# Spreading 1/rms over the partitions: transposes placed by TensorE's order in the heads and between the layers of an encoder

## The chip, the cores and the metric

The kernel runs on one NeuronCore of a Trainium2 chip. The metric is device time in microseconds for one execution, lower is better. A core has TensorE (PE: matrix products and transposes into the accumulation memory, PSUM), VectorE (DVE), ScalarE (ACT) and GpSimd (POOL) for work on rows of data, and SyncE (SP), whose queue issues nearly all DMAs here. Each engine works through its own queue in a fixed order; the engines wait for each other by semaphores.

## The reference

One encoder layer over two independent inputs of 512 tokens by 1024 channels, all in float32:

```python
x = x + 0.5 * swiglu(rms_norm(x, ffn1_norm), ffn1_w_gate, ffn1_w_up, ffn1_w_down)
h = rms_norm(x, mix_norm)
proj = h @ w_in                       # queries, keys, values, memory q k v, gates
att = gqa_block_attention(aq, ak, av)
mem = mlstm_bidirectional(mq, mk, mv, gate_pre, mlstm_gate_bias, o_pre, mlstm_head_norm)
merged = jax.nn.sigmoid(g_att) * (att @ w_up_att) + jax.nn.sigmoid(g_mlstm) * (mem @ w_up_mlstm)
x = x + merged @ w_out
x = x + 0.5 * swiglu(rms_norm(x, ffn2_norm), ffn2_w_gate, ffn2_w_up, ffn2_w_down)
return rms_norm(x, final_norm)

def rms_norm(x, g):
    y = x * lax.rsqrt(jnp.mean(x * x, axis=-1, keepdims=True) + EPS)
    return y * g
```

The mLSTM memory (4 heads of width 128, both directions) also ends in such a normalisation, per token and head: `h * rsqrt(mean(h * h) + EPS)`, times the head's gain and output gate.

## The kernel before

Data lies transposed: channels on the 128 partitions, 512 tokens along a row, so that a matrix of 1024 channels is eight tiles of 128 x 512. Both inputs ("streams" 0 and 1) are worked on together: the large products of the two feed-forward blocks and of the joint part of the input projection use seven products of half size for eight (B11, B21, T1 to T4, B22 in the code). Every float32 product is three matmuls over a high and a low part of each operand; a tile is split by a ScalarE copy (high) and a VectorE subtraction (low).

*The normalisation.* The mean of squares is over channels, that is over partitions. ScalarE squares a tile, and GpSimd or VectorE adds the eight squares into `acc`. `col_sums` (L174 to L181) turns `acc` by four TensorE transposes (L177) into a PSUM bank, so that each token has a partition, and VectorE reduces along the row (L179). `rstd_cols` adds the epsilon and takes the power -0.5, two small GpSimd steps (L165, L167). The result has one value per token, on the token's partition; to scale tiles with tokens along the row it must be spread over all partitions. `bcast_psum` (L183 to L188) does that by four more transposes (L187) of the column, broadcast to 128 x 128. `bcast_cols` copies the bank to a tile called R (L193). The banks come from a pool of two (`PT`, named pst in the profile), used in turn by all the transposes and by some products.

*The order.* The code is traced by Python in one sequence; a scheduler then gives each engine its queue, once and for all, before the kernel runs. It goes by the order of tracing as priority and by its own estimate of when each instruction's inputs are ready. `shifted(n)` sets the priority of what is traced inside it back by n (or forward, if n is negative). On the chip the queue's order does not change: TensorE stands still at an instruction whose inputs are not there, whatever waits behind it.

*Where the spreading stands.* There are fourteen. Two belong to the start of the first feed-forward block and are not touched. The others:

- R0 and R1, between the first block and the mixing part. R0 (stream 0) is made in `done1`, which the down projection `ffn_down` calls as each of its output tiles is complete (T4 gives the last tile of stream 0, then follow T1 and B22 with those of stream 1). It scales the eight tiles of stream 0 for `kv_proj` (L717). R1 is made after `k_rope` and used by `next_x1`, eight tiles along the attention loop.
- Eight memory heads, four of each stream. `mem_head` computes a head's scores (L1186, three matmuls for each of four blocks), weighs them with exponentials (ScalarE L1200, VectorE L1202), and at its end divides (L1214, L1215, L1217). `mem_out` transposes the weights (L1231), multiplies with the values (L1239), and at its end squares the result, makes the column sums, the spreading and the scaling of `og` (L1249) and splits it into `mem`. `steps` runs the two generators in turns, `mem_out` of one head against `mem_head` of the next, and calls `between` after each turn.
- R2 of both streams, between the mixing part and the second feed-forward block.

*Filler work.* Independent products are kept in units: a load (DMA, split of the weights) and a computation, run by `go` with one or two loads ahead. `first` holds the 14 units of the joint projection (24 matmuls each; two are given before `k_rope`, four among the four `q_rope` calls, the rest by `fill` in the attention loop). In the heads, `between` takes units from `queue`: the last joint product, eight merges of attention (24 matmuls), eight merges of memory (12) and eight output units (24) of stream 0. `pace` sets 7 units over the first 24 turns and 16 over the next 24.

## Time and profile before

| | |
|---|---|
| median of 3 runs | 2077.77 us (2076.35 to 2079.03) |
| the profiled execution | 2078.2 us, its span 2076.4 us |
| instructions | 27167, of them 9320 matmuls and transposes |
| DMA | 438.60 MB, 211 GB/s on average |
| granted TensorE clock, mean | 0.994 of full speed |

The span is the time from the first to the last instruction of one execution; what lies around it is the launch. In the lines of the profile PE is TensorE's matmuls and transposes, PEld its weight loads; a group is named by its line, engine and operation, and by what it writes and reads (`pst<-ident,rs` is a transpose of a tile of `rstd_cols` into a bank of `PT`). In brackets stands the idle time of the engine just before and what ended it. Where a helper is called from many places, all its calls have one line.

### The profile page before, as it was taken

Reading aid. Unit: us, or ns where it says so; the run is one execution under the profiler, and the core shown is the slowest. Engines: PE = TensorE matmul, PEld = TensorE weight load, DVE = VectorE, ACT = ScalarE, POOL = GpSimd, SP = SyncE. Lnnn points to the kernel's source line nnn. Section 1 sums busy time; section 2 is a strip of 40 time slices with the busy share of each in tenths; the row PEclk is TensorE's granted clock in tenths of the full one; section 3 lists DMA queues with packets and bytes.
Section 4 is the critical chain, followed back from the end, with each engine's and each line's share of the span. In section 5 each row is a group of like instructions: output and inputs, shape, how many; then the busy total and the mean of one; then the engine's idle time right before and its main releaser. Section 6 shows DMA issues by size and latency. Waiting matters only on the chain.

```text
span 2076.4 us, 27167 instructions
## 1 busy us (share of the span) xinstructions
PE 2036.5 (98%) x9320; PEld 1664.9 (80%) x9320; DVE 1652.3 (80%) x2802; ACT 954.3 (46%) x1763; POOL 135.4 (7%) x147
## 2 busy tenths in 40 slices
PE   8999999999999999999999998999999999999998
PEld 6888888888888777778887776878888888888887
DVE  6888888786798598669988688675888888786796
ACT  6544444442224565535555666444544444442222
POOL 1000000001002210010100110111000000000010
PEclk9999999999999999999999999999999999999999
DMA  8656555599765656664445775587656555598753
GB/s 281 198 176 198 193 172 183 189 338 365 273 214 208 204 159 206 219 205 143 139 140 165 259 229 159 170 255 218 212 175 197 193 172 183 190 347 343 274 188 117
DMA packets 332347, 438.60 MB, mean 211 GB/s; under 512 B 21072, under 2 KB 196192, under 8 KB 330416
## 3 DMA queue, kind: packets, MB, share of 16 engines
q1 hardware_dynamic: 331616, 435.60, 63.4%
q0 software_dynamic: 592, 1.27, 0.3%
q8 instruction: 73, 1.20, 0.2%
q14 instruction: 66, 0.54, 0.1%
HBM read 285.63 MB, written 151.16 MB: 210 GB/s over the span
## 4 chain that ended last, share of the span: by engine, by line
PE 86%; DVE 6%; DMA 4%; ACT 2%; issue 1%; POOL 1%; SPq 0%; DVEq 0%; POOLq 0%; ACTq 0%
PE mm L309 20%; PE pss L309 17%; PE pst L309 11%; PE mm L565 8%; PE mm L733 5%; PE pst L565 4%; PE pss L565 4%; PE mm L717 3%; PE pso L565 3%; PE pso L1059 1%; PE pst L1051 1%; PE pss L1032 1%; PE pss L717 1%; PE pst L733 1%; PE pss L1186 1%
## 5 line engine op out<-in xcount | busy, mean ns | idle before, releaser
L309 PE MATMUL mm<-xc,w 128*128 128x512 f32 x2064 | 514.2, 393 | 3.7 <-ACT w L267 2.1
L309 PEld LDWEIGHTS mm<-xc,w 128*128 128x128 f32 x2064 | 386.1, 188 | 84.6 <-ACT w L267 2.9
L309 PE MATMUL pss<-xc,w 128*128 128x512 f32 x1056 | 256.3, 391 | 0.3 <-DVE t L340 0.3
L309 PE MATMUL pst<-xc,w 128*128 128x512 f32 x1056 | 253.8, 389 | 0.0
L309 PEld LDWEIGHTS pss<-xc,w 128*128 128x128 f32 x1056 | 196.9, 188 | 47.5 <-DVE t L340 6.9
L309 PEld LDWEIGHTS pst<-xc,w 128*128 128x128 f32 x1056 | 198.2, 188 | 41.5 <-ACT t L344 0.4
L267 ACT ACTIVATE w<-t 128x512 fp32r<-128x512 f32 x232 | 141.5, 628 | 182.5 <-issue 55.2
L268 DVE TENSOR_TENSOR w<-t,w 128x512 fp32r<-128x512 f32 x232 | 157.2, 692 | 58.1 <-ACT w L267 55.7
L565 PE MATMUL mm<-rt,w 128*128 128x512 f32 (+1 forms) x819 | 189.2, 385 | 0.0
L565 PEld LDWEIGHTS mm<-rt,w 128*128 128x128 f32 x819 | 151.5, 188 | 29.7
L309 PE MATMUL pss<-xc,f 128*128 128x512 f32 x528 | 126.8, 389 | 0.0
L309 PEld LDWEIGHTS pss<-xc,f 128*128 128x128 f32 x528 | 99.1, 188 | 20.6
L634 ACT ACTIVATE w<-wr 128x512 fp32r<-128x512 f32 x72 | 45.1, 632 | 138.5 <-PE pso L565 70.9
L634 ACT ACTIVATE w<-t 128x512 fp32r<-128x512 f32 x82 | 51.6, 632 | 114.3 <-PE pst L565 69.0
L268 DVE TENSOR_TENSOR w<-wr,w 128x1024 fp32r<-128x1024 f32 x58 | 71.6, 1235 | 32.0 <-ACT w L267 31.9
L565 PE MATMUL pss<-rt,w 128*128 128x512 f32 x396 | 93.7, 389 | 0.0
L565 PE MATMUL pst<-rt,w 128*128 128x512 f32 x396 | 93.7, 389 | 0.0
L717 PE MATMUL mm<-w,xc 128*128 128x512 f32 (+1 forms) x432 | 91.2, 358 | 2.2 <-DVE xs L583 1.4
L565 PEld LDWEIGHTS pss<-rt,w 128*128 128x128 f32 x396 | 74.3, 188 | 15.4
L565 PEld LDWEIGHTS pst<-rt,w 128*128 128x128 f32 x396 | 74.3, 188 | 15.4
L267 ACT ACTIVATE w<-wr 128x1024 fp32r<-128x1024 f32 x58 | 61.4, 1058 | 50.2 <-PE pst L309 21.6
L717 PEld LDWEIGHTS mm<-w,xc 128*128 128x128 f32 x432 | 71.9, 188 | 14.1 <-DVE xs L583 1.6
(344 smaller groups left out, 3519.9 us busy)
## 6 DMA issues: line engine op xcount, KB each, us to landing
rt<-rbuf SPq DMA_DIRECT2D x154, 512.0 KB, 5.4
wr<-in_ffn_w_gate_dram SPq DMA_DIRECT2D x62, 512.0 KB, 5.5
rbuf<-tab SPq DMA_DIRECT2D x102, 256.0 KB, 4.0
wr<-in_w_in_dram SPq DMA_DIRECT2D x50, 512.0 KB, 4.7
wr<-in_ffn_w_up_dram SPq DMA_DIRECT2D x44, 512.0 KB, 4.6
rbuf<-f SPq DMA_DIRECT2D x72, 256.0 KB, 3.8
rbuf<-R SPq DMA_DIRECT2D x68, 256.0 KB, 3.9
rbuf<-t SPq DMA_DIRECT2D x66, 256.0 KB, 3.6
```

The lines of the kernel that those rows point to most:

```text
L267: pin(nc.scalar.activation(t[:, 0], src, AF.Copy))
L268: pin(V_.tensor_tensor(t[:, 1], src, f(t[:, 0]), op=ALU.subtract))
L309: nc.tensor.matmul(p, a[:, k, :], xt[:, b, k, :], start=(first and k == 0 and i == 0), stop=(k == HK_ - 1 and i == 2), skip_group_check=True)
L565: nc.tensor.matmul(p, u[:, a, d * P:(d + 1) * P], r[:, b, ts], start=(first and q == 0 and k == 0), stop=(q == len(us) - 1 and k == 2), sk ...
L634: nc.scalar.activation(hi, src, AF.Copy)
L717: nc.tensor.matmul(p[b][:, :N], a[:, bs], w_[:, kl, :], start=(k == 0 and i == 0), stop=(k == KD - 1 and i == 2))
L733: nc.tensor.matmul(p, a[:, k, :], b, start=(k == 0 and i == 0), stop=(k == n - 1 and i == 2))
L1032: nc.tensor.matmul(p, self.qT[:, h, b * P:(b + 1) * P], self.kv[:, hk * 2 + j, :], start=(j == 0), stop=(j == 1))
L1051: nc.tensor.transpose(p[:, b * P:(b + 1) * P], Ps[b][:, kb * P:(kb + 1) * P], ident)
L1059: nc.tensor.matmul(po, self.Vst[:, kv_, hk, :], w, start=(kv_ == 0 and i == 0), stop=(kv_ == 3 and i == 1))
L1186: nc.tensor.matmul(p, qk[a][:, isl], qk[b], start=(n == 0), stop=(n == 2))
```

## The change

The priority shifts around the spreading go. In their place the transposes are tied behind a given matmul of TensorE's queue: `tc.issue_after(ins)` adds, for each instruction that is traced inside it on the engine of `ins`, an edge that puts it behind `ins` in that queue; it is an order of issue, with no wait for the end of `ins`. `last_mm[0]` is the matmul traced last by `product`, `proj_w`, the down projection or a head's scores, `recent` the list of the down projection's.

In a head, the spreading, the scaling and the split become a function that is put on a list with the number 24. `passed(n)` takes n off each number on the list and runs what has come to 0. It is called with 3 after each block of scores and with 12 for each unit that `between` runs, and with 999 after the heads.

R0 moves from the last tile of stream 0 to the second tile that T1 completes, and is tied behind the fifth matmul from the end of the list. R1 moves behind the gates and one unit of `first`; among the four `q_rope` calls two units are given in place of four, so that one unit more is left to the attention loop. The sums of R2 of stream 0 move from ahead of the merges of stream 1 to behind the seventh call for one, and the spreading behind the last call; R2 of stream 1 is spread after the second unit of the new block.

```diff
+    late = []
+
+    def later(n, fn):
+        late.append([n, fn])
+
+    def passed(n=1):
+
+        for item in late[:]:
+            item[0] -= n
+            if item[0] <= 0:
+                late.remove(item)
+                with tc.issue_after(last_mm[0]):
+                    item[1]()
...
-                    nc.tensor.matmul(p, qk[a][:, isl], qk[b], start=(n == 0), stop=(n == 2))
+                    last_mm[0] = nc.tensor.matmul(p, qk[a][:, isl], qk[b], start=(n == 0), stop=(n == 2)).ins
+                passed(3)
...
             rh = rstd_cols(col_sums(h2), 4)
-            with shifted(160):
-                Rh = bcast_psum(rh)
-                V_.tensor_tensor(og, og, Rh, op=ALU.mult)
+
+            def scale():
+                V_.tensor_tensor(og, og, bcast_psum(rh), op=ALU.mult)
                 split(og, self.mem[:, h, 0, :], self.mem[:, h, 1, :])
+            later(24, scale)
...
-            with shifted(5):
-                r0 = stats(accs[0])
-            with shifted(30):
-                R0 = bcast_cols(r0)
+            r.append(stats(accs[0]))
             xc[B11], xc[B21] = xc_tile(), xc_tile()
+        if s == 1 and d == DH + 1:
+            with tc.issue_after(recent[-5]):
+                R0 = bcast_cols(r[0])
             for k in range(KD):
...
     r1 = stats(accs[1])
-    with shifted(40):
+    m0.gates()
+    go(first.pop(0), depth=2)
+    with tc.issue_after(last_mm[0]):
         R1 = bcast_cols(r1)
-    m0.gates()
...
     for b in range(4):
         m0.q_rope(b)
-        go(first.pop(0), depth=2)
+        if b % 2:
+            go(first.pop(0), depth=2)
...
-        fill(at(n + 1) - at(n))
+        n = at(n + 1) - at(n)
+        fill(n)
+        passed(12 * n)
...
-    def stats2(s):
-        r = stats(acc2[s])
-        with shifted(40):
-            R2[s] = bcast_cols(r)
-
-    stats2(0)
...
-    go(*[m1.merge_mem(d) for d in range(KD)])
+    passed(999)
+    go(*[m1.merge_mem(d) for d in range(KD - 1)])
+    r2 = stats(acc2[0])
+    go(m1.merge_mem(KD - 1))
+    with tc.issue_after(last_mm[0]):
+        R2[0] = bcast_cols(r2)
...
     up.begin(0, W[0])
-    stats2(1)
+    r2 = stats(acc2[1])
     W += [up.left(j) for j in (1, 2)]
     up.begin(1, W[1])
+    with tc.issue_after(last_mm[0]):
+        R2[1] = bcast_cols(r2)
```

## The prediction

> **What bounds the kernel now.** First the page: busy time by engine, and the chain that ended last.

> ```profile
> PE 2036.5 (98%) x9320; PEld 1664.9 (80%) x9320; DVE 1652.3 (80%) x2802; ACT 954.3 (46%) x1763; POOL 135.4 (7%) x147
> PE 86%; DVE 6%; DMA 4%; ACT 2%; issue 1%; POOL 1%; SPq 0%; DVEq 0%; POOLq 0%; ACTq 0%
> ```

> TensorE is busy for 2036.5 of 2076.4 us, so it bounds the kernel and all that can be won by waiting less is 39.9 us. Next the view of who waited for whom on TensorE (us in total, times, longest):

> ```profile
> PE pst L187 <- POOL rs L167: 12.0, 7, 4.0
> PE mm L1289 <- DMA raw<-in_x_prompt_dram: 3.6, 3, 2.1
> ```

> The largest entry by far is the change's own instruction: L187, the transposes of `bcast_psum`, waiting for GpSimd's power of -0.5. The timeline of TensorE shows the seven places (start, duration, group, and in brackets the idle time before it):

> ```profile
> 646.40 0.65 PE L187 MATMUL pst<-ident,rs 128*128 128x128 f32 x4 [1.07 <-POOL rs L167]
> 711.43 0.65 PE L187 MATMUL pst<-ident,rs 128*128 128x128 f32 x4 [1.06 <-POOL rs L167]
> 1183.48 0.47 PE L187 MATMUL pst<-ident,rs 128*128 128x128 f32 x1 [2.98 <-POOL rs L167]
> 1199.78 0.32 PE L187 MATMUL pst<-ident,rs 128*128 128x128 f32 x1 [0.45 <-POOL rs L167]
> 1262.67 0.32 PE L187 MATMUL pst<-ident,rs 128*128 128x128 f32 x1 [1.19 <-POOL rs L167]
> 1289.60 0.48 PE L187 MATMUL pst<-ident,rs 128*128 128x128 f32 x1 [3.96 <-POOL rs L167]
> 1364.88 0.32 PE L187 MATMUL pst<-ident,rs 128*128 128x128 f32 x1 [1.31 <-POOL rs L167]
> ```

> They are R0 (646), R1 (711), four of the eight memory heads (1183, 1199, 1262, 1289) and R2 of the first stream (1364): 12.02 us. The other five that the change moves (four heads and R2 of the second stream) have no such bracket. There is a second price: the view by stretches (length, busy TensorE, its weight loads, VectorE, ScalarE, GpSimd, granted clock, DMA share, GB/s) behind the three longest waits:

> ```profile
> 1179.56:1182.97 3.41, 0.94 (x5) 0.41 (x3) 3.41 (x8) 2.46 (x6) 2.32 (x3) 1.00 0.83 268
> 1182.97:1186.38 3.41, 2.90 (x11) 2.62 (x12) 1.16 (x4) 0.47 (x1) 0.46 (x1) 0.50 0.39 130
> 1261.50:1264.90 3.40, 1.54 (x10) 1.26 (x11) 2.41 (x8) 1.49 (x3) 1.12 (x1) 0.99 0.94 315
> 1264.90:1268.30 3.40, 3.14 (x11) 2.14 (x10) 2.55 (x4) 0.80 (x3) 0.00 (x0) 0.50 0.01 2
> 1285.46:1288.87 3.41, 0.18 (x1) 0.00 (x0) 3.41 (x9) 0.92 (x2) 0.59 (x2) 0.98 1.03 322
> 1288.87:1292.28 3.41, 2.68 (x10) 2.40 (x11) 1.72 (x4) 1.12 (x2) 0.67 (x1) 0.50 0.27 102
> 1292.28:1295.70 3.42, 3.42 (x11) 2.37 (x10) 3.15 (x7) 1.69 (x5) 0.00 (x0) 0.52 0.00 0
> ```

> After each of the three the granted clock is halved, for one or two stretches of about 3.4 us. TensorE is busy for 2.90 + 3.14 + 2.68 + 3.42 = 12.14 us in them; half of that, 6.1 us, is what full speed would have saved. So the ceiling of the change is 12.0 + 6.1 = 18.1 us.

> **The change part by part.** Nothing is added: the same transposes, copies and products run, and the tie is an order in TensorE's queue, not a wait. What counts is what TensorE finds next in its queue once L187 stands elsewhere.

> *Heads.* The whole tail of a head moves: four transposes, a VectorE product (L1249), a ScalarE copy and a VectorE difference (L634, L635); no DMA. The first stall:

> ```profile
> 1180.44 1.62 DVE L1215 SCALAR_TENSOR_TENSOR t<-t,dn,t 128x128 f32<-128x128 f32 x2
> 1182.18 0.34 DVE L1215 SCALAR_TENSOR_TENSOR t<-t,dn,t 128x128 f32<-128x128 f32 x1
> 1183.58 0.34 DVE L1215 SCALAR_TENSOR_TENSOR t<-t,dn,t 128x128 f32<-128x128 f32 x1
> 1185.46 0.41 PE L1231 MATMUL pst<-ident,t 128*128 128x128 f32 x1
> ```

> Behind L187 in the queue stand the L1231 transposes of the next head, which need that head's four L1215 results. The last of these ends at 1183.58 + 0.34 = 1183.92. VectorE is busy without a break in 1179.56 to 1182.97 (3.41 of 3.41 above). With L187 gone and the rest of the order kept, TensorE would wait for L1215 instead: the last L1231 starts at 1183.92 and not at 1185.46, a gain of 1.54, not 2.98. The same reading of the other three:

> ```profile
> 1200.01 0.34 DVE L1215 SCALAR_TENSOR_TENSOR f<-f,dn,f 128x128 f32<-128x128 f32 x1
> 1199.94 0.60 PE L1231 MATMUL pst<-ident,f 128*128 128x128 f32 x4
> ...
> 1262.49 0.35 DVE L1215 SCALAR_TENSOR_TENSOR t<-t,dn,t 128x128 f32<-128x128 f32 x1
> 1263.49 0.27 PE L1231 MATMUL pst<-ident,t 128*128 128x128 f32 x1
> ...
> 1288.61 0.69 DVE L635 TENSOR_TENSOR qk<-qk 128x512 fp32r<-128x512 f32 x1
> 1290.58 0.78 PE L1186 MATMUL pss<-qk 128*128 128x512 f32 x1
> ```

> At 1199 L1215 ends at 1200.35, within the group of L1231 that runs from 1199.94 to 1200.54: gain 0. At 1262 it ends at 1262.84 against a start at 1263.49: 0.65. At 1289 the L1186 behind takes the low part of k, ready at 1289.30, and started at 1290.58: 1.28. Sum 3.47. The four times four transposes now run where TensorE was busy; four cost about 0.4 us of its order (from 643.52 to 643.93 in the rows below), but they no longer stand between those L1231 and L1186; I take off 0.25 for each, half an estimate: 2.5 us stay. The bounds are 0 (everything waits as before) and 8.58, the four brackets together (the order shifts so that other matmuls fill the time). I take 2.5, since the rows above show VectorE as the next to be late.

> The results stay in time. In the first stream the last head's scale is traced two units of 24 matmuls ahead of the merge that reads it, an estimate of 10.9 us at 0.227 each (27 matmuls from 651.48 to 657.60, below); the last head of all gets its transposes right behind the last output unit, with nine matmuls of each of three merges, 6.1 us, to cover a chain that took from 1360.38 to 1363.61 (the rows under R2). Where that cover fails, TensorE waits for the rest of a chain of some 3 us, once.

> *R0.*

> ```profile
> 643.52 0.66 PE L177 MATMUL pst<-ident,R 128*128 128x128 f32 x4
> 643.93 1.40 PE L565 MATMUL mm<-rt,w 128*128 128x512 f32 x5
> 647.09 0.69 DVE L193 COPY R<-pst 128x512 f32<-128x512 f32 x1 [2.18 <-PE pst L187]
> 651.48 6.28 PE L565 MATMUL mm<-rt,w 128*128 128x512 f32 x27
> 657.60 2.20 PE L565 MATMUL pso<-rt,w 128*128 128x512 f32 x9
> 662.67 1.02 PE L717 MATMUL mm<-w,xc 128*128 128x272 f32 x6 [1.38 <-DVE xs L583]
> ```

> L187 stands 16 matmuls into the T1 products now; the new place is behind the 14th at the earliest, by trace order behind the 18th. That is two matmuls, 0.45 us, of cover at most. And VectorE cannot start the normalisation earlier; TensorE meets it again at 662.67, where it already waits 1.38 us. What is won at 646 is lost there: 0; the bounds are -0.45, if VectorE starts by so much later, and +1.07.

> *R1.* One unit of the joint projection (24 matmuls, 5.4 us) now lies between the sums and the transposes, more than the 2.88 us that the same chain took at R0, from L177 at 643.52 to L187 at 646.40, so the 1.06 goes. Against it, one of the units that lay among the four `q_rope` moves into the attention loop, with its weight fetch on SP's queue, its split on ScalarE and VectorE and its store.

> ```profile
> 716.00:824.00 108.00, 106.24 (x510) 82.19 (x508) 103.48 (x202) 69.07 (x137) 14.56 (x10) 1.00 0.61 188
> ```

> In that stretch VectorE is busy for 96% and TensorE for 98%: nearly no slack on either, DMA share 0.61. I take +1.06 and 0 for the moved unit; its bounds are -5.4 (TensorE starves for the whole unit while VectorE does rotary work) and +1.8 (TensorE's idle time there goes).

> *R2.* In the first stream the sums, with their VectorE reduction and two GpSimd steps, move behind six merges and the transposes behind the seventh; no other GpSimd work lies between.

> ```profile
> 1360.38 0.60 PE L187 MATMUL pst<-ident,rs 128*128 128x128 f32 x4
> 1362.93 0.68 DVE L635 TENSOR_TENSOR mem<-box,mem 128x512 fp32r<-128x512 f32 x1
> 1364.95 0.48 PE L733 MATMUL pst<-mem,w 128*128 128x512 f32 x1
> 1435.80 0.27 PE L187 MATMUL pst<-ident,rs 128*128 128x128 f32 x1
> ```

> What stands next is ready: the memory's last part is there at 1363.61, the merge started at 1364.95. The whole 1.31 goes (bounds 0 and 1.31). In the second stream the tie, behind the 36th matmul of the new up projection, is about where L187 runs already: 0.

> *Clock.* 0 to 6.1. Half-idle time remains at two of the three places by the reading above (from 1183.48 - 2.98 = 1180.50 to 1183.92, and from 1289.60 - 3.96 = 1285.64 to 1289.30), and the row 1261.50 shows that 1.54 busy of 3.40 was still little enough to halve the clock. I take half, 3.0.

> Sum: 2.5 + 0 + 1.06 + 1.31 + 3.0 = 7.9 us. The profiled execution took 2078.2 with a span of 2076.4; the median of the three runs is 2077.8, so the forecast is 2077.8 - 7.9 = 2069.9.

> [...]

> **Rivals.**
> 1. *The clock stays up* (0.17). If only a nearly empty stretch halves it, as 0.94 and 0.18 us busy would suggest, the shorter waits left over don't: 6.1 in place of 3.0, 2066.8. For it: two of three cases. Against it: the row 1261.50. [...]
> 2. *Nothing takes the place of the waits* (0.20): all 18.1 us, 2059.7. For it: where 24 or more matmuls happen to lie ahead of L187 (the other four heads) no wait at all is shown. Against it: VectorE's rows in the heads.
> 3. *The waits only change their name* (0.18): L1231 and L1186 stall as long, the clock falls as before; 1.06 + 1.31 remain: 2075.4. This is also the case where the change doesn't do what it says in the heads, since the tie counts matmuls and not the chain it waits for.
> 4. *Slower* (0.10): the unit moved out of the `q_rope` stretch leaves TensorE empty for 5.4 us while VectorE is full, and the attention loop, at 98%, has to take it on top: 2083.2 with nothing won elsewhere. It decides as soon as the starved time is more than what the other places give; for it speaks VectorE's 96%, against it that TensorE is handed whatever unit has its weights ready.

> The forecast has 0.35. About 4.2 us, 0.2%, is what a measurement can tell from no change. Faster: forecast, rivals 1 and 2, less the forecast's upper edge, 0.68. Same: rival 3 and that edge, 0.22. Slower: 0.10. The range runs from 2059, rival 2, to 2077, past rival 3; it leaves out rival 4 and little more.

> **What would show it.** Right: no L187 among TensorE's waits in heads, R1 and R2; in their place waits of L1231 on L1215 and of L1186 on the low part of k, 1 to 3 us each; the wait at 662 as long as before or longer; one or two stretches at half clock left. Wrong: no stretch at half clock and TensorE's idle time under 29 us (rivals 1, 2); new waits of L309 or L1032 between 715 and 825 (rival 4); L1231 stalled as long as L187 was (rival 3).

## The result, and the profile after

The changed kernel takes 2072.0 us (median; 2069.6 to 2075.9 in 17 runs) against 2076.35 us before (2072.4 to 2080.1 in 17 runs on the same chip): a ratio of 0.998, with a 95% interval of 0.9973 to 0.9988. That is 4.35 us (2.5 to 5.6 by the interval), little more than half of the 7.9 us forecast. The forecast of 2069.9 lies 2.1 us below the measured time, which is inside the range of 2059 to 2077. It came so near in part because the kernel before took 2076.35 us in this comparison and 2077.8 in the one that the forecast started from.

The profiled execution of after spans 2074.1 us against 2076.4; it is the slowest of the 17. The first row of its page:

```profile
PE 2034.7 (98%) x9320; PEld 1662.9 (80%) x9320; DVE 1653.8 (80%) x2802; ACT 953.8 (46%) x1763; POOL 133.8 (6%) x147
```

TensorE's idle time is 39.4 us; before it was 39.9. The sum hides what happened: as the stages below show, it went down where the change went after it and up elsewhere, in part where the code is the same (ahead of R0's sums it is 10.6 us against 8.9, behind the second R2 1.1 against none). The view of who waited for whom on TensorE in after (us in total, times, longest) gives the names:

```profile
PE pss L1202 <- DVE qk L636: 2.9, 2, 1.5
PE pst L187 <- POOL rs L167: 2.6, 2, 2.0
...
PE pst L1067 <- DVE f L636: 1.6, 1, 1.6
...
PE pst L1248 <- DVE t L1232: 1.2, 1, 1.2
PE mm L718 <- DVE f L636: 1.2, 1, 1.2
```

(The code moved down by 1 to 17 lines: L1231, L1215 and L1186 of before are L1248, L1232 and L1202 here, L634, L635 and L717 are L635, L636 and L718, L1051 and L1059 are L1067 and L1075, L1149 is L1165.) L187 fell from 12.0 us in seven places to 2.6 in two. The timeline of TensorE in after shows where the two are, and what stands where the others were:

```profile
647.73 0.65 PE L187 MATMUL pst<-ident,rs 128*128 128x128 f32 x4 [0.59 <-POOL rs L167]
662.77 1.02 PE L718 MATMUL mm<-w,xc 128*128 128x272 f32 x6 [0.63 <-DVE xs L584]
669.11 1.90 PE L718 MATMUL mm<-w,xc 128*128 128x272 f32 x13 [0.97 <-DVE xc L255]
786.18 0.66 PE L1067 MATMUL pst<-ident,f 128*128 128x128 f32 x4 [1.59 <-DVE f L636]
864.99 11.88 PE L718 MATMUL mm<-w,xc 128*128 128x272 f32 x75 [1.18 <-DVE f L636]
1160.70 1.19 PE L1202 MATMUL pss<-qk 128*128 128x512 f32 x4 [1.54 <-DVE qk L636]
1187.25 0.85 PE L1248 MATMUL pst<-ident,t 128*128 128x128 f32 x6 [1.22 <-DVE t L1232]
1288.39 1.42 PE L1202 MATMUL pss<-qk 128*128 128x512 f32 x4 [1.31 <-DVE qk L636]
1375.97 0.65 PE L187 MATMUL pst<-ident,rs 128*128 128x128 f32 x4 [2.01 <-POOL rs L167]
```

L187's waits for the power are gone from the heads and from R1 (711 before); the one at R0 got shorter (1.07 before, 0.59 now), the one at R2 longer (1.31 before, 2.01 now). The wait at 1160 is not new, but it was 0.77 us before. Where did the time go? Cut each trace at the same instructions: the sums of R0, of R1, the first scores of the second stream's attention, the first scores of the memory heads, the first merge, the sums of the second R2. The view by stretches of before (length, busy TensorE, its weight loads, VectorE, ScalarE, GpSimd, granted clock, DMA share, GB/s), without the first stage, the one from 949 to 1132 (183.4 us before, 183.0 after) and the last two:

```profile
643.52:708.57 65.05, 62.05 (x323) 52.31 (x324) 43.51 (x61) 36.90 (x65) 25.04 (x29) 1.00 0.76 241
708.57:949.00 240.43, 235.04 (x1163) 187.07 (x1163) 190.04 (x367) 127.61 (x256) 28.18 (x32) 1.00 0.60 191
...
1132.41:1358.34 225.93, 213.95 (x990) 170.72 (x991) 164.30 (x376) 131.96 (x302) 29.02 (x28) 0.97 0.64 206
1358.34:1430.07 71.73, 70.42 (x315) 57.33 (x314) 51.18 (x68) 29.19 (x40) 11.05 (x8) 1.00 0.73 230
```

and the same stretches of after:

```profile
644.86:709.83 64.97, 62.57 (x324) 52.45 (x324) 44.05 (x61) 36.91 (x65) 24.25 (x29) 1.00 0.76 241
709.83:954.65 244.82, 237.19 (x1164) 187.93 (x1163) 190.38 (x367) 127.59 (x256) 27.76 (x32) 0.99 0.58 188
...
1137.62:1354.02 216.40, 209.84 (x995) 168.04 (x995) 165.59 (x377) 132.19 (x303) 30.09 (x28) 0.99 0.66 216
1354.02:1426.06 72.04, 70.03 (x313) 57.17 (x311) 52.32 (x68) 28.66 (x40) 12.47 (x8) 1.00 0.73 228
```

The heads (third row) became 9.5 us shorter: 5.4 us of TensorE's idle time (225.93 - 213.95 = 11.98 before, 216.40 - 209.84 = 6.56 after) and 4.1 us of its busy time (213.95 - 209.84), since the clock fell less: its mean in these rows is 0.97 before and 0.99 after. The stage behind the sums of R1 (second row) became 4.4 us longer: 2.2 us more idle, 2.2 us more busy. R2 (last row) is 0.3 us longer. So in this pair of profiles the change earned twice what the time shows; about half was given back in the stage behind R1, and 3.2 us more were lost in two stages with the same code, ahead of R0's sums (1.3) and in the second feed-forward block (1.9). The stage ahead of R0's sums took between 640.5 and 644.9 us in the profiles of this study; that is why single spans say less here than the stages do.

The busy time that was saved in the heads is a figure of this pair alone. The profile of before has a mean granted clock of 0.994; of the 60 executions of before that stand beside the experiments only 10 have that or less, and their mean is 0.9960. The 17 of after have 0.9965. The difference, 0.0005 of 2075 us, is an estimate of what the clock gives on average: about 1 us.

### The profile page after: what moved, and what is told of

Read it like the earlier page. It is cut to its first block, busy times and chain, and to the rows that moved or that the text cites. A ratio compares the mean times of both kernels' runs of the same rounds, so it can differ in the third digit from the quotient of the medians.

```text
span 2074.1 us, 27195 instructions
## 1 busy us (share of the span) xinstructions
PE 2034.7 (98%) x9320; PEld 1662.9 (80%) x9320; DVE 1653.8 (80%) x2802; ACT 953.8 (46%) x1763; POOL 133.8 (6%) x147
## 4 chain that ended last, share of the span: by engine, by line
PE 51%; DVE 5%; DMA 3%; ACT 2%; issue 1%; POOL 1%; SPq 0%; DVEq 0%; POOLq 0%; ACTq 0%
PE mm L309 11%; PE pss L309 9%; PE pst L309 6%; PE mm L734 5%; PE mm L565 4%; PE mm L718 2%; PE pst L565 2%; PE pss L565 2%; PE pso L565 1%; PE pso L1075 1%; PE pss L1048 1%; PE pst L1067 1%; PE pst L734 1%; DMA kept<-f 1%; PE pss L718 1%
## 5 line engine op out<-in xcount | busy, mean ns | idle before, releaser
L309 PE MATMUL mm<-xc,w 128*128 128x512 f32 x2064 | 513.8, 393 | 4.6 <-ACT w L267 2.5
L309 PEld LDWEIGHTS mm<-xc,w 128*128 128x128 f32 x2064 | 386.2, 188 | 86.6 <-ACT w L267 3.2
L309 PE MATMUL pss<-xc,w 128*128 128x512 f32 x1056 | 256.3, 391 | 1.8 <-DVE t L340 1.8
L309 PE MATMUL pst<-xc,w 128*128 128x512 f32 x1056 | 253.7, 389 | 0.0
L309 PEld LDWEIGHTS pss<-xc,w 128*128 128x128 f32 x1056 | 196.8, 188 | 49.3 <-DVE t L340 8.8
L309 PEld LDWEIGHTS pst<-xc,w 128*128 128x128 f32 x1056 | 198.2, 188 | 41.1
L565 PE MATMUL mm<-rt,w 128*128 128x512 f32 (+1 forms) x819 | 189.2, 385 | 0.0
L565 PEld LDWEIGHTS mm<-rt,w 128*128 128x128 f32 x819 | 151.5, 188 | 29.7
L309 PE MATMUL pss<-xc,f 128*128 128x512 f32 x528 | 126.8, 389 | 0.0
L309 PEld LDWEIGHTS pss<-xc,f 128*128 128x128 f32 x528 | 99.1, 188 | 20.6
L635 ACT ACTIVATE w<-wr 128x512 fp32r<-128x512 f32 x72 | 45.2, 632 | 137.7 <-PE pso L565 72.0
L635 ACT ACTIVATE w<-t 128x512 fp32r<-128x512 f32 x82 | 51.5, 632 | 114.5 <-PE pst L565 69.2
L718 PE MATMUL mm<-w,xc 128*128 128x512 f32 (+1 forms) x432 | 93.0, 363 | 3.1 <-DVE f L636 1.2
L565 PE MATMUL pst<-rt,w 128*128 128x512 f32 x396 | 93.7, 389 | 0.0
L565 PE MATMUL pss<-rt,w 128*128 128x512 f32 x396 | 93.7, 389 | 0.0
L565 PEld LDWEIGHTS pst<-rt,w 128*128 128x128 f32 x396 | 74.3, 188 | 15.4
L565 PEld LDWEIGHTS pss<-rt,w 128*128 128x128 f32 x396 | 74.3, 188 | 15.4
L718 PEld LDWEIGHTS mm<-w,xc 128*128 128x128 f32 x432 | 73.6, 193 | 15.9 <-DVE xc L255 1.8
```

The costliest lines, as they stand in the source:

```text
L309: last_mm[0] = nc.tensor.matmul(p, a[:, k, :], xt[:, b, k, :], start=(first and k == 0 and i == 0), stop=(k == HK_ - 1 and i == 2), skip_g ...
L565: last_mm[0] = nc.tensor.matmul(p, u[:, a, d * P:(d + 1) * P], r[:, b, ts], start=(first and q == 0 and k == 0), stop=(q == len(us) - 1 an ...
L635: nc.scalar.activation(hi, src, AF.Copy)
L718: nc.tensor.matmul(p[b][:, :N], a[:, bs], w_[:, kl, :], start=(k == 0 and i == 0), stop=(k == KD - 1 and i == 2))
```

## The experiments

Each ratio is against the kernel before on the same chip. Diffs are against the changed kernel unless said otherwise. "Sums to scores" is the stretch from the sums of R0 to the first scores of the memory heads: 488.9 us before and 492.8 after.

**The heads alone.** All of the change's edits at R0, R1 and R2 are taken back; `later`, `passed` and the tie of `scale` stay.

```
-            r.append(stats(accs[0]))
+            with shifted(5):
+                r0 = stats(accs[0])
+            with shifted(30):
+                R0 = bcast_cols(r0)
...
     r1 = stats(accs[1])
-    m0.gates()
-    go(first.pop(0), depth=2)
-    with tc.issue_after(last_mm[0]):
+    with shifted(40):
         R1 = bcast_cols(r1)
+    m0.gates()
...
-    go(*[m1.merge_mem(d) for d in range(KD - 1)])
     r2 = stats(acc2[0])
-    go(m1.merge_mem(KD - 1))
-    with tc.issue_after(last_mm[0]):
+    with shifted(40):
         R2[0] = bcast_cols(r2)
+    go(*[m1.merge_mem(d) for d in range(KD)])
...
     r2 = stats(acc2[1])
+    with shifted(40):
+        R2[1] = bcast_cols(r2)
...
```

> Only the heads' part of the change; R0, R1 with its units, and R2 stand as before. Theory A (in the heads a shorter wait for VectorE is left, and most half-speed time goes; the loss lies in the attention loop): between the first scores of the memory heads and the first merge of the second stream 9 to 10 us less than before, nothing lost ahead of it, ratio to before 0.9954 +- 0.001. Rival B (the heads give only what the prediction gave them, 2.5 + 3.0 us): 0.9974. In the trace both leave one wait of the L1215 kind and one for the low part of k.

Measured: 2064.1 us, ratio 0.9955 (0.9941 to 0.9968). It beats the whole change; theory A holds, and rival B's 0.9974 lies outside. The same kernel again, later, as the base of the last group:

> The heads part alone once more, with the next three runs on one chip, as their base: 0.9955 as before (0.9941 to 0.9968), some 2065 us.

2064.7 us, 0.9959 (0.9947 to 0.9971). Two stages of its view by stretches, from the sums of R1 and from the first memory scores:

```profile
706.40:947.44 241.04, 236.28 (x1163) 188.06 (x1163) 189.80 (x367) 127.51 (x256) 28.89 (x32) 0.99 0.58 191
...
1130.69:1344.91 214.22, 207.78 (x995) 166.91 (x995) 166.17 (x377) 132.23 (x303) 29.86 (x28) 1.00 0.67 218
```

In the heads the clock is 1.00 throughout, and TensorE is busy 213.95 - 207.78 = 6.2 us less than before: about the 6.1 us that the prediction had as the price of the half clock in its one profile. The stage behind R1 is back at 241.0. So by the two ratios the heads part is worth some 9 us (8.5 and 9.3), and the rest of the change costs about 5. Over its ten executions the mean clock is 0.9968, 0.0008 above before: by the same estimate up to 1.7 us of the 9 come from the clock on average, and the idle time (11.98 before, 214.22 - 207.78 = 6.44 here) gives 5.5. Together that is 7.2 us, inside the interval of the second ratio (6 to 11 us).

**The R1 part taken back** (the rest as in the change; all four units of work lie among the `q_rope` again).

```
     r1 = stats(accs[1])
-    m0.gates()
-    go(first.pop(0), depth=2)
-    with tc.issue_after(last_mm[0]):
+    with shifted(40):
         R1 = bcast_cols(r1)
+    m0.gates()
...
-        if b % 2:
-            go(first.pop(0), depth=2)
+        go(first.pop(0), depth=2)
```

> The change without its R1 part: R1 spread ahead of the gates with the old shift, four units among the four q_rope calls again. Theory A (the rearranged units cost about 4 us in the attention loop and behind it): ratio to before 0.996, 4 us less than the whole change, and the first scores of the memory heads about 4 us earlier than in the changed kernel. Rival C (what the attention loop lost is the scatter of one profiled run): 0.998 as the whole change.

2068.3 us, 0.9971 (0.9959 to 0.9982). The interval holds theory A's 0.996 and rival C's 0.998, so the time does not decide between them. Sums to scores took 487.9 us, 4.9 less than in the change, as theory A has it.

**Only the moved unit put back.**

```
     for b in range(4):
         m0.q_rope(b)
-        if b % 2:
+        if b:
             go(first.pop(0), depth=2)
```

> The change with three units among the q_rope calls instead of two, so that the attention loop has as many units as before; R1 stays tied behind the gates and one unit. Theory A1 (the unit more in the attention loop is what costs): as without the R1 part, 0.996. Rival A2 (the later R1, or the order of gates and unit, costs): 0.998, as the whole change.

2072.0 us, 0.9989 (0.998 to 0.9998); sums to scores 492.6 us, as in the change. Theory A1's 0.996 is out: the moved unit isn't what costs.

**More cover at R2.** The sums stand one merge earlier, so that two merges, 24 matmuls, lie between them and the transposes.

```
-    go(*[m1.merge_mem(d) for d in range(KD - 1)])
+    go(*[m1.merge_mem(d) for d in range(KD - 2)])
     r2 = stats(acc2[0])
-    go(m1.merge_mem(KD - 1))
+    go(*[m1.merge_mem(d) for d in (KD - 2, KD - 1)])
```

> The change with the sums of R2 of the first stream one merge earlier, so that 24 matmuls instead of 12 lie between them and the spreading. Theory A: the wait of 2.0 us of L187 at R2 goes and nothing takes its place, ratio to before 0.997. Rival D (VectorE, full there, makes another product late): the wait of L187 goes and one of 1 to 2 us appears behind it, 0.998.

2067.4 us, 0.9966 (0.9954 to 0.9979): 0.0014 below the change, about as much as both intervals together leave uncertain. TensorE's timeline of this kernel at R2:

```profile
1361.77 0.60 PE L177 MATMUL pst<-ident,R 128*128 128x128 f32 x4
1362.13 3.02 PE L734 MATMUL pst<-mem,w 128*128 128x512 f32 x12
1364.98 2.88 PE L734 MATMUL pss<-mem,w 128*128 128x512 f32 x12
1367.70 0.60 PE L187 MATMUL pst<-ident,rs 128*128 128x128 f32 x4
```

No bracket is left, nor does a wait appear behind it up to the sums of the second R2, as rival D had it. Twelve matmuls take about 3 us, and the chain takes longer, as the timeline of the change itself shows (TensorE, VectorE and GpSimd, in order of time):

```profile
1370.60 0.60 PE L177 MATMUL pst<-ident,R 128*128 128x128 f32 x4
...
1370.80 0.69 DVE L1130 SCALAR_TENSOR_TENSOR t<-t,pst 128x512 f32<-128x512 f32 x1 [0.16 <-PE pst L734]
1371.40 0.68 DVE L636 TENSOR_TENSOR ml<-t,mh 128x512 fp32r<-128x512 f32 x1
1372.01 0.68 DVE L1131 TENSOR_TENSOR t<-t,t 128x512 f32<-128x512 f32 x1
1372.61 0.68 DVE L179 TENSOR_REDUCE cs<-pst 128x4 f32<-128x512 f32 x1
...
1373.38 1.13 POOL L165 TENSOR_SCALAR rs<-cs 128x4 f32<-128x4 f32 x1 [21.45 <-DVE cs L179]
1374.60 1.33 POOL L167 TENSOR_TENSOR rs<-rs,nhalf 128x4 f32<-128x4 f32 x1
```

The sums leave TensorE at 1371.20, but VectorE's reduction L179 starts only at 1372.61, behind three instructions of the merge; GpSimd's two steps end at 1375.93, and L187 starts at 1375.97. From L177 to L187 that is 5.37 us. GpSimd has a part in it too. In the heads alone, where the reduction starts 0.63 us after L177 and not 2.01, the same chain takes 2.82 us, and its first GpSimd step is this:

```profile
1349.42 0.23 POOL L165 TENSOR_SCALAR rs<-cs 128x4 f32<-128x4 f32 x1 [6.59 <-DVE cs L179]
```

So of the 2.55 us that the chain is longer at its new place, 1.4 are VectorE's lateness and 1.2 the two GpSimd steps (0.23 and 1.04 us there, 1.13 and 1.33 here). Why these take longer here no run shows.

**Why does the R1 part cost?** With the moved unit out, two theories were left, the order of the gates (T1) and a late R1 (T2). First R1 late, with everything else of that part as in the kernel before:

```
     r1 = stats(accs[1])
-    m0.gates()
-    go(first.pop(0), depth=2)
-    with tc.issue_after(last_mm[0]):
+    with shifted(300):
         R1 = bcast_cols(r1)
+    m0.gates()
...
         m0.q_rope(b)
-        if b % 2:
-            go(first.pop(0), depth=2)
+        go(first.pop(0), depth=2)
```

> Heads, R0 and R2 as in the change; the R1 part undone (gates emitted after R1, four units of work among the q_ropes), but the spread of R1 pushed much later in priority: 62 matmuls stand between its sums and its transposes (5 in the kernel before, 23 in the change). Theory T1: what the R1 part costs is the order of the gates, which the change emits ahead of the spread; then the stretch from the sums of R0 to the first memory scores takes 488 us as without the R1 part, and the ratio is that of the run without it, 0.997. Rival T2: it costs because R1 itself comes late, and with it the rows of x1 that the second mixer's projections read; then the stretch takes 493 us or more (492.8 in the change), and the ratio is 0.998 to 0.9995.

2083.7 us, 1.004 (1.0026 to 1.0054); sums to scores 505.2 us. A late R1 is dear, and the order of the gates can't be all that costs here; that it costs nothing is not shown. Then R1 early, with the gates behind it and three units:

```
     r1 = stats(accs[1])
-    m0.gates()
     go(first.pop(0), depth=2)
     with tc.issue_after(last_mm[0]):
         R1 = bcast_cols(r1)
+    m0.gates()
...
-        if b % 2:
+        if b:
```

> The change with R1 tied behind the unit of work as there, but the gates emitted after R1, and three units among the q_ropes: 5 matmuls stand between the sums and the transposes, as in the kernel before, and one unit still stands ahead of the q_ropes. T1 (order of the gates) and T2 (R1 late) both expect the 488 us of the stretch from the sums of R0 to the memory scores back, ratio 0.997. A third theory, T3, that the unit ahead of the q_ropes costs by itself, expects 492 to 493 us and 0.998 to 0.999 as in the run with three units.

2079.2 us, 1.0018 (1.0009 to 1.0026); sums to scores 500.1 us. As sole explanations all three theories fall with this: R1 is as early as before, and the stretch is 7 us longer than in the change. Its timeline (ScalarE, VectorE, TensorE) shows a stall that none of them had:

```profile
746.93 0.60 ACT L780 ACTIVATE t<-mm 128x512 f32<-128x512 f32 x1 [4.38 <-DMA j_o<-t]
747.43 0.71 ACT L635 ACTIVATE f<-f 128x256 fp32r<-128x256 f32 x2
747.87 1.07 DVE L636 TENSOR_TENSOR f<-f,f 128x256 fp32r<-128x256 f32 x2 [3.86 <-ACT f L635]
748.75 0.41 PE L981 MATMUL pst<-ident,f 128*128 128x128 f32 x2 [4.02 <-DVE f L636]
```

ScalarE waits 4.38 us for a store of the joint projection (`j_o<-t`) to free its buffer. Behind it in ScalarE's order stands the split of a rotary result (L635), VectorE's half of the split (L636) waits for that, and TensorE's transposes for VectorE. So an early R1 does not make the stretch short by itself; the order in which the engines find their other work counts as well. How much of the 7 us this one stall explains was not tested. The last runs measured the parts by themselves instead.

**The parts, one by one on top of the heads.** Each of these is the heads alone plus one of the change's other parts as it stands there; the diffs are against the heads alone. R1:

```
     r1 = stats(accs[1])
-    with shifted(40):
+    m0.gates()
+    go(first.pop(0), depth=2)
+    with tc.issue_after(last_mm[0]):
         R1 = bcast_cols(r1)
-    m0.gates()
...
-        go(first.pop(0), depth=2)
+        if b % 2:
+            go(first.pop(0), depth=2)
```

> The heads part and the R1 part (gates ahead, the tie, one unit moved), R0 and R2 as in the kernel before. If the R1 part is what gives back the gain of the heads, 0.997 to 0.998 (3 to 5 us over the heads alone), and the stretch from the sums of R0 to the first memory scores takes 492 us against 488. Rival: that stretch scatters by as much from run to run (another kernel with R1 as in the kernel before took 491.6 there), and the ratio is that of the heads alone, 0.9955.

2068.7 us, 0.9976 (0.9967 to 0.9985); sums to scores 491.2 us against 489.3 in its base. That is 0.0017, or 3.5 us, over 0.9959, and the rival's 0.9955 is out. R2 (the second stream's likewise, behind `up.begin(1, W[1])`):

```
+    go(*[m1.merge_mem(d) for d in range(KD - 1)])
     r2 = stats(acc2[0])
-    with shifted(40):
+    go(m1.merge_mem(KD - 1))
+    with tc.issue_after(last_mm[0]):
         R2[0] = bcast_cols(r2)
-    go(*[m1.merge_mem(d) for d in range(KD)])
```

> The heads part and the R2 parts as in the change (12 matmuls of cover), R0 and R1 as in the kernel before. From the runs without R1 (0.9971) and with 24 matmuls of cover (0.9966 against 0.998): 0.0005 to 0.0014 over the heads alone, 0.996 to 0.997. Rival: the R2 parts are worth nothing either way, 0.9955.

2067.7 us, 0.9972 (0.9964 to 0.9981): 0.0013 over the base. The intervals overlap, so the time alone does not show a cost; TensorE's timeline shows the wait, 0.98 us in the base:

```profile
1371.69 0.65 PE L187 MATMUL pst<-ident,rs 128*128 128x128 f32 x4 [2.40 <-POOL rs L167]
```

R0:

```
-            with shifted(5):
-                r0 = stats(accs[0])
-            with shifted(30):
-                R0 = bcast_cols(r0)
+            r.append(stats(accs[0]))
             xc[B11], xc[B21] = xc_tile(), xc_tile()
+        if s == 1 and d == DH + 1:
+            with tc.issue_after(recent[-5]):
+                R0 = bcast_cols(r[0])
```

> The heads part and the R0 part, R1 and R2 as in the kernel before. The forecast put R0 at nothing (its wait stays, 0.45 us before and 0.59 us after): the ratio of the heads alone, 0.9955, within 0.001. Rival: x0 comes later by the two added matmuls and the first projections of the mixer wait, as before the row at 662; then 0.996 to 0.997.

2066.6 us, 0.9964 (0.9951 to 0.9977): no difference that can be told.

**All but the heads.** The heads go back to `shifted(160)`; R0, R1 and R2 as in the change.

```
-            def scale():
-                V_.tensor_tensor(og, og, bcast_psum(rh), op=ALU.mult)
+            with shifted(160):
+                Rh = bcast_psum(rh)
+                V_.tensor_tensor(og, og, Rh, op=ALU.mult)
                 split(og, self.mem[:, h, 0, :], self.mem[:, h, 1, :])
-            later(24, scale)
```

> The change with its heads part undone (the spread of 1/rms in the eight memory heads by priority as in the kernel before); R0, R1 and R2 as in the change. If the parts add up as the earlier runs say (heads alone 0.9955, everything 0.998), the rest costs 0.0025: ratio 1.0025 (1.001 to 1.004), some 2079 us, slower than the kernel before. The forecast's own terms for the rest (R1 1.1 us, R2 1.3 us, R0 nothing, part of the clock) expect a gain: 0.9985, 2071 us.

2078.4 us, 1.0008 (0.9999 to 1.0017). Without the heads no gain is left: the forecast's own terms, 0.9985, lie outside. The loss that adding the parts led to expect is not clear either: 0.0008 is just below its least, 0.001, and the interval reaches from none to 0.0017.

**What earned something, together.** The heads, and the first R2 with 24 matmuls of cover; R0, R1 and the second R2 as in the kernel before. Against the heads alone:

```
+    go(*[m1.merge_mem(d) for d in range(KD - 2)])
     r2 = stats(acc2[0])
-    with shifted(40):
+    go(*[m1.merge_mem(d) for d in (KD - 2, KD - 1)])
+    with tc.issue_after(last_mm[0]):
         R2[0] = bcast_cols(r2)
-    go(*[m1.merge_mem(d) for d in range(KD)])
```

> Only what earned something: heads as in the change, R0, R1 and the second R2 as in the kernel before, and the first R2 tied with 24 matmuls of cover (sums two merges ahead of the end). Additive theory: heads alone 0.9955, less the 1.1 us by which the stretch from the first merge to the sums of the second R2 is shorter with 24 matmuls of cover than before's way in heads alone (69.8 against 70.9): 0.995, 2065 us, and below heads alone. Rival: before's way of R2 stalls no more than that in fast stretches, so 0.9955 and no difference that can be told.

2065.6 us, 0.9949 (0.9937 to 0.9962), the lowest ratio of all and 0.003 below the change; from the heads alone it can't be told apart. R2 shows no wait here either. Its stretch from sums to scores took 491.6 us, though its code there, and in the trace the order of each engine's instructions behind the sums of R1, is that of the heads alone (487.6 and 489.3): so much does this stretch scatter, and 3 us of it in a single profile prove nothing by themselves. Over all profiles it took 491.0 to 492.8 us with R1 tied behind the gates (four kernels) and 487.4 to 491.6 with R1 as before (seven).

**Where R1's cost sits.** Not by an experiment, but by the traces: VectorE's waits between 700 and 960 us of the heads alone have this row,

```profile
DVE st L1170 <- POOL R L1165: 2.4, 3, 1.2
```

and those of the heads with the R1 part this one:

```profile
DVE st L1170 <- POOL R L1165: 4.1, 4, 1.6
```

The four profiles with R1 tied behind the gates (the change, the moved unit put back, more cover at R2, and this one) have 3.9 to 4.5 us here, the kernel before and the six with R1 as in it 1.3 to 2.5. The two slowest kernels do not follow this row: the late R1 has 2.5, the gates behind R1 3.6, so it is not all that makes this stretch long. TensorE's idle time from the sums of R1 to the memory scores is 6.9 to 9.7 us in the four, and 4.6 to 6.1 in before and five of the six; the sixth, the kernel of the last experiment above, has 7.9. L1170 is a maximum over the rows of the memory's gates (`mem_max`), which GpSimd prepares (L1165) from a row that a DMA brings. The timeline of the heads with the R1 part at the longest one (GpSimd, VectorE, TensorE):

```profile
779.14 1.29 POOL L1165 TENSOR_TENSOR R<-R,tab 128x512 f32<-128x512 f32 x1 [5.56 <-DMA R<-ebuf]
780.47 0.69 DVE L1170 TENSOR_REDUCE st<-R 128x4 f32<-128x512 f32 x1 [1.57 <-POOL R L1165]
781.07 0.68 DVE L636 TENSOR_TENSOR f<-pst,f 128x512 fp32r<-128x512 f32 x1
781.81 0.66 PE L1067 MATMUL pst<-ident,f 128*128 128x128 f32 x4 [1.02 <-DVE f L636]
```

VectorE, the fullest engine beside TensorE in this stage (busy for 190.07 of the 243.17 us behind the sums of R1), stands idle for 1.57 us at the head of its order, for a maximum that the memory heads read only after this attention; the split that TensorE needs (L636) stands behind it, and TensorE waits 1.02 us. In the kernel before VectorE waits there too, 1.22 us at 784.34, but that split does not stand behind the maximum. The 1.59 us at 786.18 in the change is the same place. In the kernel before, TensorE's waits for these transposes (L1051 there) are 0.35 us at most.

## Why the prediction was right, and where it was not

The time came near the forecast because two errors of opposite sign met, and because the kernel before was 1.4 us faster than in the forecast's reference. That is luck. By its own steps:

- **The ceiling** of 18.1 us was not passed. L187's 12.0 us went to 2.6. The 6.1 us of half clock came back whole between one profile of before and one of the heads alone, but they are the price of one execution in which the clock fell more than in most; as an average they are too high.
- **Heads, 2.5 us, measured 5.4** (TensorE's idle time there). The mechanism was right, down to the places: L1248 waits for L1232 at 1187, L1202 for the low part of k at 1288. The term was mis-sized. At 1288 the prediction left 3.96 - 1.28 = 2.68 us of wait, and 1.31 stayed. The reading kept the rest of the order fixed, but with L187 elsewhere the order moved: more transposes of the next head (L1248), a matmul of its scores (L1202) and two of the values (L1256) now stand ahead of the wait. TensorE has work until 6.3 us after the start of the head's column sums (L177, 1280.78 to 1287.08), where it ran dry after 2.9 before (1282.70 to 1285.64), while the low part of k comes later, 7.55 us after them in place of 6.60. And the 0.25 us taken off for each of four groups of transposes was not seen. Rival 3 (the waits only change names) is out, and so is rival 2: 6.56 us of idle time stay in the heads.
- **Clock, 3.0 us, measured 4.1 in the heads of this pair of profiles**, less what a new stretch at half speed costs in the stage behind R1; by the mean clock of 60 and 17 executions it is about 1 us. So the term was mis-sized: it was taken from one execution of before, and whether a wait costs the clock differs from one to the next (last section). The view by stretches of after around the two that are left:

```profile
862.35:865.76 3.41, 1.88 (x12) 1.46 (x13) 3.29 (x6) 3.41 (x8) 0.00 (x0) 1.00 1.02 342
865.76:869.17 3.41, 3.41 (x18) 3.41 (x18) 3.38 (x6) 1.39 (x5) 0.00 (x0) 0.52 1.03 386
...
1285.65:1289.06 3.41, 1.76 (x8) 1.20 (x9) 3.41 (x7) 0.63 (x1) 1.26 (x2) 1.00 0.48 168
1289.06:1292.47 3.41, 3.41 (x10) 2.68 (x9) 3.41 (x7) 2.05 (x6) 0.00 (x0) 0.52 0.01 2
```

  The first row of each pair holds the wait, the second runs at half speed (0.52) and costs about 1.7 us, an estimate: half of its 3.41 us of busy time. Rival 1 (only a nearly empty stretch halves the clock) is out for the change: TensorE was busy for more than half of both first rows.
- **R0, 0: right.** Its wait fell to 0.59 us. The wait at 662 got shorter as well (0.63 against 1.38), not "as long as before or longer"; those behind it got longer (0.97 and 0.17 against 0.51). Together the waits are 0.6 us less, yet the stage takes 64.97 us against 65.05, and the part alone can't be told from none.
- **R1, +1.06 us and 0 for the moved unit: this step failed.** The wait at 711 went, as said, but the part costs 3.5 us (0.9976 against 0.9959; with both intervals, some 0.5 to 6.5); taking it back from the change gave 0.9971 against 0.998, the same way but within the noise. Of the unit itself the 0 was right. What the step left out, as far as the traces show it, is that VectorE, busy for 96% from 716 to 824 us, has its work in a fixed order, and that emitting the gates and R1 elsewhere reorders it (a wait of 1.57 us for L1170 ahead of TensorE's 1.02, above): the row of 96% was read as no slack for the unit, not as a price for any new order. Rival 4 had the stretch right and the mechanism wrong; its sign of new waits of the joint projection or of the attention's scores did not appear, the waits are L1067's and L718's.
- **R2, +1.31 us: this failed too.** The step looked only at what stands behind the wait and set no cover against the chain from the sums to the transposes. One merge of 12 matmuls is 2.7 us at the prediction's own 0.227 each, less than the 2.88 that the chain took at R0. Behind a running merge it took 5.37, over a cover of 3; the wait grew to 2.0 us. For the second stream the 0 was right: neither profile shows a wait there.

So 5.5 us were forecast for heads and clock, and some 9 came; 2.4 were forecast for R1 and R2, and together the parts beside the heads cost about 5 instead. That R1 costs is clear of noise by little; that R2 costs shows only as a longer wait in the traces. What stays open: the other parts without the heads cost 0.0008 where one by one on top of them they cost 0.0005 + 0.0017 + 0.0013 = 0.0035. Each of these is uncertain by about 0.0015, and whether the clock falls differs from run to run (below), so the parts need not add. And which of the gates and of R1's place makes VectorE's order worse was not separated. The rows of L1170 are 1.7 us longer with the R1 part, half of its 3.5; that this is its cause is a reading and not shown by a run.

## What to carry to other kernels

- Where a stall is replaced by the next one in the queue, read the ends of the next waits for the bound, but expect the orders to move as well: in the heads 2.5 us were forecast so and 5.4 came. What a shorter stall saves of the clock is read from the mean clock of many executions, not from one profile: here 4.1 us in one pair and about 1 us on average.
- Cover for a chain through other engines is counted in time, against the chain as it runs at the new place among the work there: 12 matmuls for 5.4 us left a wait, 24 left none.
- Where a second engine is full, a reordering can have a price that the stall removed does not show. Take such changes one part at a time: here one part of four earned everything, and the others together gave half of it back.

## What the hardware showed unasked

The same wait was followed by half of TensorE's clock in one run and by the full clock in another. The heads alone ran twice; at R1 both have the same instructions and the same idle time. First run, by stretches and then TensorE's timeline:

```profile
706.32:709.73 3.41, 2.33 (x17) 1.82 (x16) 1.22 (x2) 0.60 (x1) 1.27 (x2) 1.00 0.76 231
709.73:713.14 3.41, 3.41 (x22) 2.74 (x22) 2.54 (x7) 1.14 (x3) 0.00 (x0) 1.00 0.02 5
```

```profile
708.46 0.65 PE L187 MATMUL pst<-ident,rs 128*128 128x128 f32 x4 [1.08 <-POOL rs L167]
...
710.20 2.34 PE L309 MATMUL mm<-xc,w 128*128 128x512 f32 x9
```

Second run, the same:

```profile
708.40:711.81 3.41, 2.55 (x20) 2.42 (x21) 1.31 (x3) 0.00 (x0) 0.80 (x1) 1.00 0.59 188
711.81:715.22 3.41, 3.41 (x12) 2.29 (x11) 1.69 (x4) 1.25 (x3) 0.00 (x0) 0.50 0.00 0
```

```profile
709.26 0.65 PE L187 MATMUL pst<-ident,rs 128*128 128x128 f32 x4 [1.07 <-POOL rs L167]
...
711.00 3.51 PE L309 MATMUL mm<-xc,w 128*128 128x512 f32 x9
```

The nine matmuls take 2.34 us in the one and 3.51 in the other, and from the sums of R0 the second run reaches the scores 1.7 us later. So too in the heads: the wait of L1202 at 1288 is 1.30 or 1.31 us in the change and in the eleven experiments that have the new heads, and half speed followed it in four of these twelve.

The stretches of this section are cut along this grid. So cut, the four of twelve in the heads stand apart: the stretch that holds most of the wait had TensorE busy for 1.70 to 1.94 us in the four, and for 2.00 to 2.61 us in the other eight. But the busy time of the stretch does not decide it by itself. At R1 half speed followed 2.55 us in the second run and not 2.33 in the first, and at R2, in the kernel with the moved unit put back, full speed followed 1.53 us (1372.80 to 1376.21). What else it depends on no run here shows. A nearly empty stretch was not needed for it: half speed followed stretches with 1.70 to 2.55 us of TensorE's work in 3.41.
